# Dilated attention on one TensorE: projection steps paced by an estimate of each half slot's work, instruction pins from the first slot, and later merge pieces

## The chip, the cores and the metric

The kernel runs on 1 core of one Trainium2 chip. The metric is the time of one execution in microseconds (us). Three timed runs of the kernel before gave 2720.28, 2725.63 and 2730.9 us; the median is 2725.63.

The engines by the names of the profile: PE is TensorE (matrix products and transposes), PEld its weight loads, DVE is VectorE, ACT is ScalarE, POOL is GpSimd, and SP is the engine whose queue issues most transfers.

## The reference, cut to what matters

Two layers of a decoder trunk, on 1024 positions by 1024 features in f32. Layer 0 mixes tokens with a gated MLP, layer 1 with the attention below; each is followed by a dense MLP. The change lies in the attention: 16 heads of 64 features and three patterns (window, dilation), whose outputs are weighted by a softmax over their log sums.

```python
B_PATTERNS = ((128, 1), (512, 4), (2048, 16))
def dilated_branch(q, k, v, window, dilation, slopes):
    ...
    s = jnp.einsum('bnqrhe,bnkrhe->bnrhqk', qb, kb, preferred_element_type=jnp.float32) * (E ** -0.5)
    ...
    s = s + bias
    s = jnp.where(valid[None, :, None, None], s, NEG)
    m = jnp.max(s, axis=-1, keepdims=True)
    p = jnp.exp(s - m)
    l = jnp.sum(p, axis=-1, keepdims=True)
    o = jnp.einsum('bnrhqk,bnkrhe->bnqrhe', p / l, vb.astype(jnp.float32))
    lse = (m + jnp.log(l))[..., 0].transpose(0, 1, 4, 2, 3)
    ...
def mixer_b(h, w_qkv, w_out, slopes):
    qkv = (h @ w_qkv).reshape(B, S, N_PAT, 3, B_HEADS, B_HEAD_DIM)
    ...
    wts = jax.nn.softmax(jnp.stack(lses, axis=0), axis=0)[..., None]
    o = jnp.sum(wts * jnp.stack(outs, axis=0), axis=0)
    return o.reshape(B, S, B_HEADS * B_HEAD_DIM).astype(h.dtype) @ w_out
```

## The kernel before, in words

Every f32 operand of a product is split into a high and a low part, and a product is three matmuls (high by high, high by low, low by high). `split` casts the high part on ACT and subtracts the low part on DVE.

The stages follow one another: the gated MLP, an MLP, `values` (all value projections and those q and k that go through memory, L1338), `attention`, its output projection `go_on`, and the last MLP. `attention` works on 8 pairs of heads, and in each pair on the patterns 2, 1, 0 in this order: 24 groups, with a name such as `sc_0_1` or `pv_2_0` for pattern 0 or 2.

The order of work is written out by hand. `slots` is a table of 202 slots of two half slots each, 16 half slots a group. `at(slot, pos, rank)` and `in_half(half_slot, rank)` put closures in. The loop at the end of `attention` walks the half slots and runs what stands there. For one group these are:

- `scores` (L1553): 6 to 24 small matmuls into two `sc` banks, one for each head; two banks of each of the kinds `sc`, `pv`, `mm` and `tr` exist;
- `soften` (DVE: adds the bias and takes the row's extreme, into `p` and `stat`) and `exponentials` (ACT);
- `transposes` (L1612, L1615) into a `tr` bank; `halve` (ACT, `pThi`) and `low` (DVE, `pTlo`), its split;
- `weighted` (L1644): products with the values into a `pv` bank; `gather` (ACT) and `join` (DVE) bring it into `oT` and free the bank;
- `statistics` (L1684 to L1693): stores `stat` to memory (`st_dram`).

For each pair `merge` then reads the statistics back (`read`, L1705, into `mst`), forms the weights (`factors`, `weights`, L1732 to `w_dram`), loads them spread over the partitions (`spread`, L1739, `bc`), and scales, adds and splits the three `oT` in twelve pieces, two halves each. Pairs 0 to 5 store the result in `o_dram` (L1766). `rows_first` (L1809) and `rows_second` (L1816) load it again for the output projection, whose first steps (`out_begin`, L1829) run in the last slots, six for every eight half slots, from slot `last_group - 8` on.

Between the slots' own work the loop puts steps of `project()`: one step is three matmuls of 512 columns (L1455), 384 steps in all, that make q and k of pattern 2 and k of pattern 1 for the coming groups from the layer's input. `load` fetches a weight (L1432, `wq_raw`, `wk_raw`, two buffers), `cut` splits it (`wqk_hi` on ACT, `wqk_lo` on DVE), and a finished block is split into `qhi`, `qlo`, `khi`, `klo` one half slot later. 40 lead steps run ahead of the first slot. Then a credit gives (368 - 40)/326, about 1.006 step for each of the first 326 half slots, whatever stands in them, and 16/25 of a step for each one after.

While `in_order[0]` is true, instructions that go through `V` (DVE) and `A` (ACT) are pinned: they run in the order in which the program writes them. PE, SP and POOL are left to a scheduler that places each instruction when its inputs are ready by its own model. `in_order[0]` is set ahead of the lead steps.

## Time and profile before

| | |
|---|---|
| median of three runs | 2725.63 us (2720.28 to 2730.9) |
| the profiled execution | 2721.97 us, span 2720.3 us |
| mean granted TensorE clock | 0.993 |
| PE busy | 2653.1 us (98%), 13194 matmuls |
| DVE, ACT busy | 2016.9 us (74%), 1394.3 us (51%) |
| attention: first projection matmul to last weighted sum | about 1460 to 2022 us of the span |

A share of the whole span says little about a stage that takes a fifth of it. For this change the rows to read are those of the attention alone: the idle time of PE stretch by stretch, the waits behind it, and the clock in each stretch. A timeline row gives the start, the duration of one instruction or of a run of equal ones (x12), and in brackets the idle time just before it with the instruction that ended it. Matmuls are pipelined, so what one costs is the distance from its start to the next start, not its own duration.

### The profile page before, as it was taken

The page shows a single profiled execution, that of the slowest core. Times are in us where ns is not written, and L with a number is a line of the kernel's source. Part 1 is how long each engine was busy: PE and PEld are TensorE (multiplying, and loading weights), DVE is VectorE, ACT ScalarE, POOL GpSimd, SP SyncE. Part 2 cuts the span into 40 slices and gives each one's busy share as a digit, 9 for nine tenths or more (in the row PEclk, how much of TensorE's full clock was granted, in tenths as well). Part 3 has the DMA queues.
Part 4 walks back from the last instruction along what each step waited for, and adds up shares of the span by engine and source line. Part 5 has one row for each costly group of instructions (what it writes and reads, how often), then busy time and mean ns, then how long its engine had stood idle before and what let it go on. Part 6 is the DMA issues. An engine that isn't in the chain of part 4 may idle for free.

```text
span 2720.3 us, 37241 instructions
## 1 busy us (share of the span) xinstructions
PE 2653.1 (98%) x13194; PEld 2191.1 (81%) x13194; DVE 2016.9 (74%) x3652; ACT 1394.3 (51%) x2621; POOL 130.5 (5%) x211
## 2 busy tenths in 40 slices
PE   6999999999999999999999999999999999999998
PEld 5788888888888877888887888888787888878887
DVE  6787697877888778666663677777768966577887
ACT  3354475555444464444443677777645655544332
POOL 1000000000000001111111000000010000000000
PEclk9999999999999999999999999999999999999999
DMA  7534346677967756666646366667892654495562
GB/s 264 161 120 131 116 141 213 224 224 249 341 223 250 240 166 199 240 216 220 213 170 195 109 172 174 167 172 186 253 224 90 213 186 158 148 315 184 171 208 87
DMA packets 342223, 525.76 MB, mean 193 GB/s; under 512 B 52572, under 2 KB 169732, under 8 KB 342036
## 3 DMA queue, kind: packets, MB, share of 16 engines
q1 hardware_dynamic: 323060, 455.21, 53.2%
q0 software_dynamic: 18976, 68.17, 6.8%
q8 instruction: 104, 1.70, 0.3%
q14 instruction: 83, 0.68, 0.1%
HBM read 376.93 MB, written 146.36 MB: 192 GB/s over the span
## 4 chain that ended last, share of the span: by engine, by line
PE 66%; DVE 12%; issue 11%; DMA 6%; ACT 4%; POOL 1%; SPq 0%; DVEq 0%; POOLq 0%; ACTq 0%
PE psv L1338 15%; PE psd L972 11%; PE psua L813 8%; PE psk L1455 5%; PE psuc L813 4%; DMA adaw<-in_ada_w_dram 3%; PE psd_wout L404 3%; PE psq L1455 3%; PE psu L383 3%; PE sc L1553 3%; PE pv L1644 3%; DVE adaacc L51 2%; PE psub L813 2%; PE psv L485 1%; PE pT L1612 1%
## 5 line engine op out<-in xcount | busy, mean ns | idle before, releaser
L813 PE MATMUL psua<-right,left 128*128 128x512 f32 x1536 | 365.7, 392 | 0.1
L972 PE MATMUL psd<-rhi,lhi 128*128 128x512 f32 x896 | 350.3, 391 | 3.0 <-ACT part L51 3.0
L972 PE MATMUL psd<-rlo,lhi 128*128 128x512 f32 x896 | 350.0, 391 | 0.2
L972 PE MATMUL psd<-rhi,llo 128*128 128x512 f32 x896 | 349.6, 390 | 0.0
L813 PEld LDWEIGHTS psua<-right,left 128*128 128x128 f32 x1536 | 288.9, 189 | 61.7 <-DVE right L51 1.2
L51 ACT ACTIVATE p<-p,stat 128x128 f32<-128x128 f32 (+1 forms) x384 | 169.5, 443 | 68.1 <-DVE stat L51 67.0
L972 PEld LDWEIGHTS psd<-rhi,lhi 128*128 128x128 f32 x896 | 169.0, 189 | 39.0 <-ACT part L51 3.9
L972 PEld LDWEIGHTS psd<-rlo,lhi 128*128 128x128 f32 x896 | 168.8, 188 | 35.7 <-DVE rlo L51 1.1
L972 PEld LDWEIGHTS psd<-rhi,llo 128*128 128x128 f32 x896 | 168.9, 189 | 35.5
L813 PE MATMUL psuc<-right,left 128*128 128x512 f32 x768 | 187.1, 390 | 0.0
L51 DVE TENSOR_TENSOR pTlo<-pT,pThi 128x512 fp32r<-128x512 f32 (+1 forms) x160 | 99.5, 622 | 102.4 <-ACT pThi L51 101.0
L51 DVE SCALAR_TENSOR_TENSOR adaacc<-adaw,silu_c,adaacc 128x512 f32<-128x512 f32 x168 | 128.6, 774 | 56.1 <-DMA adaw<-in_ada_w_dram 55.0
L813 PEld LDWEIGHTS psuc<-right,left 128*128 128x128 f32 x768 | 143.6, 188 | 29.8 <-DVE right L51 0.2
L51 ACT ACTIVATE part<-part 128x512 f32<-128x512 f32 x224 | 141.4, 632 | 49.8 <-DVE part L51 44.6
L51 DVE TENSOR_TENSOR left<-ws,left 128x512 fp32r<-128x512 f32 x128 | 87.8, 687 | 73.8 <-ACT left L51 72.0
L51 DVE TENSOR_TENSOR llo<-lraw,lhi 128x1024 fp32r<-128x1024 f32 x112 | 136.3, 1217 | 2.2 <-ACT lhi L51 2.2
L1455 PE MATMUL psk<-form_L,wqk_hi 128*128 128x512 f32 x384 | 131.0, 422 | 0.0
L51 ACT CAST left<-ws 128x512 fp32r<-128x512 f32 x128 | 79.1, 620 | 96.8 <-DVE ws L51 96.6
L51 ACT CAST lhi<-lraw 128x1024 fp32r<-128x1024 f32 x112 | 117.3, 1047 | 10.5 <-PE psd L972 3.3
L51 ACT CAST pThi<-pT 128x512 fp32r<-128x512 f32 (+1 forms) x160 | 84.6, 529 | 72.8 <-PE pT L1612 57.6
L1338 PE MATMUL psv<-vrhi,form_S 128*128 128x512 f32 x384 | 120.1, 391 | 1.8 <-DVE vpart L51 0.9
L1338 PE MATMUL psv<-form_S,vrhi 128*128 128x512 f32 x384 | 118.3, 389 | 0.0
(322 smaller groups left out, 6093.4 us busy)
## 6 DMA issues: line engine op xcount, KB each, us to landing
lraw<-forms SPq DMA_DIRECT2D x112, 512.0 KB
adaw<-in_ada_w_dram SPq DMA_DIRECT2D x192, 256.0 KB
up<-in_mlp_w_up_dram SPq DMA_DIRECT2D x64, 512.0 KB
forms<-s SPq DMA_DIRECT2D x128, 256.0 KB
rraw<-in_mlp_w_down_dram SPq DMA_DIRECT2D x64, 512.0 KB
vraw<-in_b_w_qkv_dram SPq DMA_DIRECT2D x50, 512.0 KB
forms<-part SPq DMA_DIRECT2D x96, 256.0 KB
v<-vs POOLq DMA_DIRECT2D x48, 512.0 KB, 4.5
```

Of the source, the lines that this page charges most:

```text
L51: ins = call(*a, **k)
L383: T.matmul(dst, s[a], m[b], start=(n == 0), stop=(n == last))
L404: T.matmul(p[:], stat[a][:, k, o : o + P], u[b][:, w], start=n == 0, stop=n == count - 1)
L485: T.matmul(sums[u, half][:], units[u][a_][:, k * P : (k + 1) * P], hT[half][b_][:, k, :], start=k == 0 and a_ + b_ == 0, stop=k == KD - 1 ...
L813: T.matmul(acc, w[:, a, k, :], right[p][:, b, k, :], start=p in (1, 2, 5) and k + a + b == 0, stop=k == 3 and a == 1, skip_group_check=True)
L972: ins = T.matmul(sums[kind, m][:], l[a][:, k, m * P : (m + 1) * P], r[b][:, k, :], start=p in (1, 5, 2, 3) and kp + k + a + b == 0, stop=k ...
L1338: T.matmul(acc, rows[:, m * P : (m + 1) * P], cols_, start=p in (1, 2, 5) and kp + k + a + b == 0, stop=kp == 1 and k == 1 and a == 1, ski ...
L1455: T.matmul(p[:], wu[a][:, k * P : (k + 1) * P], h_op(k, half, b), start=k + c_ == 0, stop=k == KD - 1 and c_ == 2)
L1553: T.matmul(banks[e][:, sl], q_[a][rows, tq], k_[b][rows, keys], start=c_ == 0, stop=c_ == 2)
L1612: T.transpose(pst[:, o : o + P], probs[t][:, P : 2 * P] if has[t] else probs[t][:, 0:P], ident[:])
L1644: T.matmul(pvs[b][:, q0 % HALF : q0 % HALF + w_], stt, x_[:, o_ : o_ + w_], start=not begun[b], stop=left[b] == 0, skip_group_check=True)
```

## The change

Four things change, all in `attention`; no instruction is added or removed.

1. The steps' pace. `scores`, `transposes` and `weighted` add an estimate of their TensorE time to `spent[0]` as they are written. Each half slot adds 1.325 less `spent[0]` to the credit, and a step costs 0.7: heavy half slots get no step or one, light ones two.
2. `in_order[0]` is set behind the lead steps, so the lead's casts and subtracts aren't pinned.
3. In `merge`, `read` moves from slot `base + 1` to `base + 2`, `spread` from `base + 6` to `base + 8`, and each split becomes two pieces, "high" (ACT) and "low" (DVE and the store); the pieces' half slots are a new list, and for pair 6 they begin two half slots later.
4. `rows_first` and `rows_second` move three half slots earlier.

```diff
--- before.py
+++ after.py
@@ -1411,6 +1411,7 @@
             def h_op(k, half, part):
                 return form[f"L{1 if half else 2}{1 + k // 4}"][:, part, k % 4, :]
 
+            spent = [0.0]
             late = []
 
             def leave():
@@ -1540,6 +1541,7 @@
                             G.tensor_scalar(st["bias"][:], (far if g == 2 else near)[:],
                                             -8.0 * DILATION[g] * 2.0 ** (-8.0 * (h + 1) / N_HEADS), 1.0, ALU.mult, ALU.mult)
                     banks, used, spans = [bank("sc", f"sc_{2 * hp + e}_{g}_{m}") for e in range(2)], 0, []
+                    spent[0] += 0.29 + sum(0.42 if has[t] else 0.35 for t in groups[m])
                     for t in groups[m]:
                         w = 2 * P if has[t] else P
                         sl = slice(used, used + w)
@@ -1609,6 +1611,7 @@
                     def transposes(m, h=h, probs=probs, packs=packs, pT=pT):
                         pst = bank("tr", f"pT_{h}_{g}_{m}")
                         for t, nxt, o in packs[m]:
+                            spent[0] += 0.11 * (1 + nxt)
                             T.transpose(pst[:, o : o + P], probs[t][:, P : 2 * P] if has[t] else probs[t][:, 0:P], ident[:])
                             end = o + P
                             if nxt:
@@ -1630,6 +1633,7 @@
 
                     def weighted(m, e=e, h=h, rows=rows, packs=packs, pT=pT, pvs=pvs, st=st):
                         begun, left = st["begun"], st["left"]
+                        spent[0] += 0.1 + sum(0.114 * (1 + nxt) for _, nxt, _ in packs[m])
                         for t, nxt, o in packs[m]:
                             stt = my["v"][:, t, 2 * e : 2 * e + 2, :].rearrange("p a c -> p (a c)")
                             for x_ in pT[m]:
@@ -1698,7 +1702,7 @@
                 base = 8 * (3 * hp + 3)
                 box = {}
 
-                @at(*((base + 1, 1) if hp < N_PAIRS - 1 else (base - 1, 0)))
+                @at(*((base + 2, 1) if hp < N_PAIRS - 1 else (base - 1, 0)))
                 def read():
                     box["st"] = st = qp.tile([P, 3, 2, 16], F32, name=f"mst_{hp}", tag="mst", bufs=1)
                     for g in range(3):
@@ -1731,7 +1735,7 @@
                     for g in range(3):
                         nc.sync.dma_start(w_dram[hp, g].rearrange("e (q n) -> q e n", n=NT), a[:, g].rearrange("p (e n) -> p e n", n=NT))
 
-                @at(*((base + 6, 1) if hp < N_PAIRS - 1 else (base + 1, 1)))
+                @at(*((base + 8, 1) if hp < N_PAIRS - 1 else (base + 1, 1)))
                 def spread():
                     for g in (1, 2, 0):
                         bc = box[g] = row_bc(f"bc_{hp}_{g}")
@@ -1760,18 +1764,21 @@
                         hi, lo = (box[i][:, w].bitcast(F32R) for i in (2, 1))
                     else:
                         hi, lo = (t[:, hp, :] for t in ending["oT"][half])
-                    split(hi, lo, box[0][:, w])
+                    if g == "high":
+                        A.copy(hi, box[0][:, w])
+                        return
+                    V.tensor_tensor(lo, box[0][:, w], hi, op=ALU.subtract)
                     if hp < N_PAIRS - 2 and half:
                         for i in range(2):
                             nc.sync.dma_start(o_dram[hp, :, i, :], box[2 - i][:])
 
-                pieces = ((scale, 2), (scale, 1), (scale, 0), (add, 2), (add, 1), (cut, 0))
+                pieces = ((scale, 2), (scale, 1), (scale, 0), (add, 2), (add, 1), (cut, "high"), (cut, "low"))
                 if hp == N_PAIRS - 1:
                     ending["merge"] = [lambda f=f, g=g, half=half: f(g, half) for half in range(2) for f, g in pieces]
                     return
                 steps = [lambda f=f, g=g, half=half: f(g, half) for f, g in pieces for half in range(2)]
                 for n, f in enumerate(steps):
-                    in_half(2 * base + ((23, 25, 29, 31, 35, 36, 39, 40, 43, 47, 49, 53)[n] if hp < N_PAIRS - 2 else n + 22), 4)(f)
+                    in_half(2 * base + ((25, 29, 31, 35, 36, 39, 40, 43, 47, 48, 49, 50, 51, 54)[n] if hp < N_PAIRS - 2 else n + 24), 4)(f)
 
             for hp in range(N_PAIRS):
                 oTs = {}
@@ -1801,14 +1808,14 @@
             for k, half_slot in ((0, -64), (1, -56), (3, -48), (2, -38), (4, -33), (7, 11), (5, 17), (6, 18)):
                 in_half(2 * last_group + half_slot, 4)(lambda k=k: load_unit(k))
 
-            @at(last_group - 9, 0)
+            @at(last_group - 11, 1)
             def rows_first():
                 ending["oT"] = [act_pair("oTs_0")]
                 for i, t in enumerate(ending["oT"][0]):
                     for c in range(3):
                         nc.sync.dma_start(t[:, 2 * c : 2 * c + 2, :].bitcast(F32), o_dram[2 * c : 2 * c + 2, :, i, 0:HALF].rearrange("k p t -> p k t"))
 
-            @at(last_group - 8, 1)
+            @at(last_group - 9, 0)
             def rows_second():
                 ending["oT"].append(act_pair("oTs_1"))
                 for i, t in enumerate(ending["oT"][1]):
@@ -1867,19 +1874,20 @@
 
             stream = project()
             lead, credit = 5 * KD, 0
-            in_order[0] = True
             for n in range(lead):
                 leave()
                 next(stream)
+            in_order[0] = True
             due = 0
             for n, slot in enumerate(slots):
                 for half_of, pos in enumerate(slot):
                     for _, f in sorted(pos, key=lambda x_: x_[0]):
                         f()
                     leave()
-                    credit += (368 - lead) * 25 if 2 * n + half_of < 326 else 16 * 326
-                    while credit >= 326 * 25:
-                        credit -= 326 * 25
+                    credit += 1.325 - spent[0]
+                    spent[0] = 0.0
+                    while credit >= 0.35:
+                        credit -= 0.7
                         next(stream, None)
                     if n >= last_group - 8:
                         due += 6
```

What that does to the order shows at three places. The first is ACT at the start of the attention. `qs` are splits of the last blocks of `values` (from PSUM banks `psv` or sums `vpart`), `wqk_hi` the casts of the first projection weights; + marks the order after, - the order before:

```order
 L51 CAST qs_1_4_2_11876<-psv_0_1_2_11474 128x512
+L51 CAST wqk_hi<-wq_2_raw 128x1024
+L51 CAST wqk_hi<-wk_2_raw 128x1024
 L51 CAST qs_1_4_3_11892<-psv_0_1_3_11491 128x512
 L51 CAST qs_1_3_0_11909<-vpart_1_6_0_11685 128x512
 L51 CAST qs_1_3_1_11926<-vpart_1_6_1_11703 128x512
 L51 CAST qs_1_3_2_11943<-vpart_1_6_2_11724 128x512
+L51 CAST wqk_hi<-wk_1_raw 128x1024
+L51 CAST wqk_hi<-wq_2_raw 128x1024
 L51 CAST qs_1_3_3_11960<-vpart_1_6_3_11742 128x512
-L51 CAST wqk_hi<-wq_2_raw 128x1024
-L51 CAST wqk_hi<-wk_2_raw 128x1024
```

The first two weight casts no longer stand behind all `qs` casts but ahead of the last five, and two further weight casts stand ahead of the last one.

The second is TensorE in the middle of the attention, behind the score block `sc_0_1` of the third pair. Before:

```order
L1553 MATMUL sc_0_1_14489<-bk_1_14328,bq_1_14326 128x256
L1455 MATMUL psk_2_0_14433<-form_L_8626,wqk_hi 128x512 x2
L1455 MATMUL psk_2_0_14433<-form_L_8626,wqk_lo 128x512
L1644 MATMUL pv_1_0_14510<-pThi_1_0_14457,v_1_14109 128x256
L1644 MATMUL pv_1_0_14510<-pTlo_1_0_14458,v_1_14109 128x256
L1644 MATMUL pv_1_0_14510<-pThi_1_0_14457,v_1_14109 128x128
L1644 MATMUL pv_1_0_14510<-pTlo_1_0_14458,v_1_14109 128x128
```

After:

```order
L1555 MATMUL sc_0_1_14532<-bk_1_14363,bq_1_14361 128x256
L1648 MATMUL pv_1_0_14550<-pThi_1_0_14497,v_1_14130 128x256
L1648 MATMUL pv_1_0_14550<-pTlo_1_0_14498,v_1_14130 128x256
L1648 MATMUL pv_1_0_14550<-pThi_1_0_14497,v_1_14130 128x128
L1648 MATMUL pv_1_0_14550<-pTlo_1_0_14498,v_1_14130 128x128
L1456 MATMUL psk_1_1_14422<-form_L_8187,wqk_hi 128x512 x2
L1456 MATMUL psk_1_1_14422<-form_L_8187,wqk_lo 128x512
```

The half slot of a score block gets no projection step now, so the weighted sum follows the scores directly and the step comes behind it. The step itself is of another weight (`psk_1_1` against `psk_2_0`), as the paces differ.

The third is TensorE where the projection ends. Before, its last matmuls stand in the last pair, behind transposes and weighted sums of its pattern 2 and ahead of `sc_1_0` of pattern 1:

```order
L1455 MATMUL psk_1_0_18375<-form_L_8626,wqk_hi 128x512 x2
L1455 MATMUL psk_1_0_18375<-form_L_8626,wqk_lo 128x512
L1644 MATMUL pv_2_0_18541<-pThi_2_0_18494,v_2_18246 128x128
L1644 MATMUL pv_2_0_18541<-pTlo_2_0_18495,v_2_18246 128x128
```

After, they stand in pair 6, behind `sc_0_2` and ahead of the score block `sc_0_3` of its pattern 0:

```order
L1456 MATMUL psk_1_0_18081<-form_L_8626,wqk_hi 128x512 x2
L1456 MATMUL psk_1_0_18081<-form_L_8626,wqk_lo 128x512
L1648 MATMUL pv_1_1_18187<-pThi_1_3_18182,v_1_17698 128x256
L1648 MATMUL pv_1_1_18187<-pTlo_1_3_18183,v_1_17698 128x256
L1648 MATMUL pv_1_1_18187<-pThi_1_3_18182,v_1_17698 128x128
L1648 MATMUL pv_1_1_18187<-pTlo_1_3_18183,v_1_17698 128x128
L1555 MATMUL sc_0_3_18229<-bk_3_18148,bq_3_18146 128x256
```

So the stretch from there to `sc_1_0` of the last pair, about 20 half slots, has no projection step any more, and the output projection's steps begin where they did.

## The prediction

> **What bounds the kernel now.** The page's first part says it: busy time, share of the span and instructions per engine.
>
> ```profile
> PE 2653.1 (98%) x13194; PEld 2191.1 (81%) x13194; DVE 2016.9 (74%) x3652; ACT 1394.3 (51%) x2621; POOL 130.5 (5%) x211
> ```
>
> TensorE (PE) is the bound; the change leaves its 13194 matmuls as they are, so it can only take away TensorE's idle time and slow spells, or add to them. All that it moves lies in the attention, which runs from the last value projection to the last weighted sum. I cut that part into stretches with the windows view: length, busy time by engine (PE, PEld, DVE, ACT, POOL), granted clock, DMA share, GB/s.
>
> ```profile
> 1457.80:2022.00 564.20, 555.46 (x3817) 466.48 (x3818) 400.14 (x1275) 380.11 (x1134) 32.54 (x58) 0.99 0.66 182
> 1460.30:1463.80 3.50, 3.50 (x9) 2.77 (x10) 2.34 (x2) 0.81 (x1) 2.30 (x3) 0.56 0.90 269
> 1500.00:1920.00 420.00, 417.69 (x2964) 352.86 (x2963) 319.63 (x1031) 297.34 (x905) 20.07 (x40) 1.00 0.61 169
> 1927.40:1968.00 40.60, 37.53 (x270) 31.12 (x269) 27.11 (x101) 27.71 (x89) 1.40 (x4) 0.96 0.83 264
> 1951.50:1955.00 3.50, 3.50 (x13) 3.12 (x14) 3.28 (x23) 2.62 (x13) 0.11 (x1) 0.52 0.78 283
> 1962.00:2022.00 60.00, 59.05 (x377) 48.78 (x376) 36.24 (x106) 40.01 (x110) 8.24 (x10) 1.00 0.91 227
> ```
>
> In 564.20 us TensorE idles 564.20 - 555.46 = 8.74 us, and in two spells it is busy at about half its clock: 3.50 x (1 - 0.56) = 1.5 us and 3.50 x (1 - 0.52) = 1.7 us are lost there. So **11.9 us, 0.44% of the kernel, is all the idle time and lost clock that the attention has**. The waits of PE name the pieces (total, times, longest):
>
> ```profile
> PE pv L1644 <- DVE oT L51: 3.2, 7, 1.2
> PE psq L1455 <- ACT wqk_hi L51: 2.4, 1, 2.4
> PE sc L1553 <- DVE klo L51: 0.9, 1, 0.9
> PE sc L1553 <- DMA bk<-qk: 0.6, 1, 0.6
> ```
>
> 2.4 us lie at the start, 420.00 - 417.69 = 2.3 in the 420 us of the middle, 40.60 - 37.53 = 3.1 in the 40 us before the last pair's second pattern, and 60.00 - 59.05 = 0.95 behind it. I now price the change at these four places.
>
> **Start: the pins begin behind the lead steps (-3.9).** The timeline (start, duration, engine, what, idle before and its releaser):
>
> ```profile
> 1460.21 1.22 PE L1455 MATMUL psq<-form_L,wqk_hi 128*128 128x512 f32 x2 [2.42 <-ACT wqk_hi L51]
> ...
> 1447.91 0.59 ACT L51 CAST qs<-psv 128x512 fp32r<-128x512 f32 x1 [2.33 <-DMA qk<-qs]
> 1458.59 0.62 ACT L51 CAST qs<-vpart 128x512 fp32r<-128x512 f32 x1 [2.10 <-DVE vpart L51]
> 1459.12 1.04 ACT L51 CAST wqk_hi<-wq_raw 128x1024 fp32r<-128x1024 f32 x1
> 1460.19 1.23 DVE L51 TENSOR_TENSOR wqk_lo<-wq_raw,wqk_hi 128x1024 fp32r<-128x1024 f32 x1 [0.25 <-ACT wqk_hi L51]
> 1416.86 0.37 SPq L1432 DMA_DIRECT2D wq_raw<-in_b_w_qkv_dram  x1
> ```
>
> The first projection matmul waits 2.42 us for a cast of 1.04 us that is pinned behind the last `qs` cast, though its weights were asked for at 1416.86. In the changed order the first two wqk_hi casts stand on ACT directly ahead of the `qs` cast of 1447.91, where ACT idled 2.33 us; 2 x 1.04 = 2.1 fits, and DVE idles beside it. The 2.42 us go. The half clock of 1460.30 to 1463.80 begins right behind that idle, so I let its 1.5 us go too. What is late next: the two further casts now stand ahead of the last `qs` cast and can hold it by up to 2 x 1.04, less the 2.10 that ACT idled there: nothing reaches PE, since the blocks made of that `qs` are read by scores far later. Bounds: -3.9, and 0 if another cast takes the place.
>
> The Trainium skill, "TensorE: Matmul & The Clock Gate", Part 1 ("What's actually happening" and "HAM oscillation"), has the clock fall to a half after an idle window of about 3.4 us, and warns only of gaps longer than that. By that rule the 2.42 us gap would not be what halved the clock, and the sum would end 1.5 us higher. The row agrees with the half clock and its length of some 3.4 us, but shows it behind 2.42 us, and the spell of 1951.50 begins behind a gap of 1.23 (row of 1950.16 below).
>
> **Middle: steps chosen by what a half slot leaves (-0.1).** Idle time first: 2.3 us in 420 us, mostly `pv` behind the last `oT` join (the row of waits above), once on a block load, and behind it a score block once on DVE.
>
> ```profile
> 1667.69 0.98 PE L1553 MATMUL sc<-bk,bq 64*128 64x256 f32 x12 [0.63 <-DMA bk<-qk]
> 1931.53 1.32 PE L1553 MATMUL sc<-bk,bq 64*128 64x256 f32 x12 [0.22 <-DVE stat L51]
> ```
>
> Filling light half slots more and heavy ones less gives a `pv` block more matmuls between it and the join that frees its bank, but it brings score blocks closer to the softens that free theirs. I take -1.3 (half of 2.3 goes), with bounds of -2.3 and +3: one 0.22 wait as at 1931.53 in each of 8 pairs is 1.8, and a doubled block wait 0.63 more.
>
> Then the order itself has a price, inside PE's busy time: what a matmul takes depends on its neighbour.
>
> ```profile
> 1531.46 0.98 PE L1553 MATMUL sc<-bk,bq 64*128 64x256 f32 x12
> 1532.36 0.72 PE L1455 MATMUL psk<-form_L,wqk_hi 128*128 128x512 f32 x2
> 1532.93 0.39 PE L1455 MATMUL psk<-form_L,wqk_lo 128*128 128x512 f32 x1
> ...
> 1464.29 0.62 PE L1455 MATMUL psq<-form_L,wqk_hi 128*128 128x512 f32 x2
> 1464.75 0.39 PE L1455 MATMUL psq<-form_L,wqk_lo 128*128 128x512 f32 x1
> 1503.17 0.22 PE L1644 MATMUL pv<-pThi,v 128*128 128x128 f32 x1
> 1503.23 0.27 PE L1644 MATMUL pv<-pTlo,v 128*128 128x128 f32 x1
> 1503.34 0.28 PE L1644 MATMUL pv<-pThi,v 128*128 128x128 f32 x1
> 1504.02 0.68 PE L1455 MATMUL psq<-form_L,wqk_hi 128*128 128x512 f32 x2
> 1504.54 0.39 PE L1455 MATMUL psq<-form_L,wqk_lo 128*128 128x512 f32 x1
> 1927.43 0.97 PE L1553 MATMUL sc<-bk,bq 64*128 64x256 f32 x12
> 1928.34 0.39 PE L1644 MATMUL pv<-pThi,v 128*128 128x256 f32 x1
> 1928.56 0.28 PE L1644 MATMUL pv<-pTlo,v 128*128 128x256 f32 x1
> ```
>
> From start to start, a pair of projection matmuls takes 1464.75 - 1464.29 = 0.46, behind scores 0.57 (+0.11), behind `pv` 0.52 (+0.06). A `pv` takes 1503.34 - 1503.23 = 0.11, behind scores 0.22 (+0.11), and 0.06 as the first of the narrow pattern behind a projection (-0.05). In the changed order scores are followed by a projection 17 times instead of 63 and by `pv` 53 instead of 6; `pv` follows a projection 93 times instead of 143, a projection follows `pv` 116 instead of 133, and scores are entered 81 times instead of 74. So: -46 x 0.11 = -5.1; +47 x 0.11 = +5.2; -17 x 0.06 = -1.0; -50 x (0 to -0.05) = 0 to +2.5, of which I take 0.6, as only the narrow pattern's first one gains; 7 more entries into scores, which no row shows apart: 0.11 behind each and, I assume, as much ahead of it, +1.5, from 0 to double. Sum +1.2, bounds -0.9 and +4.6. Middle: -1.3 + 1.2 = -0.1.
>
> **Tail: the filler runs out earlier (+2).** Before, the last projection matmul starts at 1957.23; in the changed order it stands ahead of the last score block of pair 6, some 20 half slots earlier, while the output projection's steps still begin where they did. How much filler leaves that stretch, the same window of the projection's line (L1455) says:
>
> ```profile
> 1927.40:1968.00 40.60, 14.81 (x45) 7.95 (x45) 0.96 0.83 264
> ```
>
> 45 matmuls, at 0.46 / 2 = 0.23 each, are 10.3 us of PE. Without them PE has 37.53 - 10.3 = 27.2 us of work there, DVE 27.11 and ACT 27.71: three engines that pass each block to one another, with nothing left to hide a handover. PE's work as a whole doesn't change, so only the stretch's idle time counts: at least 27.7 - 27.2 = 0.5 us, at most all that was filled, 40.6 - 27.2 = 13.4 us. The nearest row is the same stretch with its filler, where 3.1 us still were lost and 1.7 at half clock:
>
> ```profile
> 1950.16 0.30 PE L1644 MATMUL pv<-pThi,v 128*128 128x128 f32 x1 [1.23 <-DVE oT L51]
> 1957.23 0.40 PE L1455 MATMUL psk<-form_L,wqk_lo 128*128 128x512 f32 x1
> 1960.34 0.33 PE L1553 MATMUL sc<-klo,qhi 64*128 64x128 f32 x2 [0.93 <-DVE klo L51]
> ```
>
> The 0.93 goes: the last `klo` is split long before its scores. The 1.23 waits for a join on DVE; pair 6's merge pieces, which share DVE there, start two half slots later, which I expect to move that wait rather than to remove it. I take 7 us, near the middle and above the 4.8 of before: +2, bounds -4 and +8.6. The two loads of finished rows (L1809, L1816) go out three half slots earlier each, behind pair 5's last store, which moves one half slot later; the tiles are needed only by the output projection behind 1961, so I cost them at nothing. If they do hold SP's queue, what waits behind them is the last pair's blocks, and a late block cost 0.63 us at 1667.69.
>
> **Merge's moves (0).** Its splits keep their casts (ACT) and subtracts (DVE), now in two half slots, so DVE no longer waits in order for the cast; no instruction is added. Its read stands in SP's queue behind the `st_dram` store that it waits for:
>
> ```profile
> 1655.77 0.37 SPq L1689 DMA_DIRECT2D st_dram<-stat  x1
> 1662.25 0.36 SPq L1705 DMA_DIRECT2D mst<-st_dram x1
> 1662.70 0.69 SPq L1520 DMA_DIRECT2D bq<-qk  x1
> ...
> SPq L1432 <- DVE wqk_lo L51: 69.0, 15, 13.2
> ```
>
> 6.5 us pass there and the block loads go out behind it; the 0.63 us at 1667.69 come from this. The new order keeps store, read and block loads in this sequence, so nothing goes.
>
> **The sum.** -3.9 - 0.1 + 2 = -2.0, so 2721.97 - 2.0 = 2720.0 for an execution like the profiled one. That one lies 3.7 under the median of the three runs (2725.63) and 2.7 under the mean of all four (2724.6); runs of one program differ by 10.6 us, so I add 2.7: **2723**.
>
> **The rivals.**
>
> *Every stall goes.* If DVE and ACT, relieved by merge's later pieces, keep pace without filler, the tail keeps 0.5 to 2 us and the start and middle give all: -3.9 - 2.3 + 1.2 - 4 = -9.0, so 2724.6 - 9.0 = 2716; with the switches at their lower bound, 2714. For it: no engine has more than 27.71 us there. Against it: the joins were late even with filler.
>
> *Nothing changes.* TensorE's work is conserved, and waits only change places: 2724.6. For it: 0.55% idle in the middle leaves pacing nothing to earn.
>
> *The block loads come late in every pair (slower).* In the changed SP order a `wk_raw` load stands between merge's read and the `bq`/`bk` loads. It must wait for the subtract that frees its buffer; such waits took 69.0 / 15 = 4.6 us each, and a block load had no slack at 1667.69. If that subtract comes after the read, 8 pairs lose up to 4.6 us each; with half of it covered, 8 x 2.3 = 18, or 8 x (2.3 + 1.5) = 30 if each gap also halves the clock: 2723 + 18 = 2741 to 2753. Against it: ACT's and DVE's new order has that cut earlier, so the buffer should be free. It decides once the subtract ends after the read's issue.
>
> *The tail's upper bound.* All 13.4 us idle, some with half clock behind: +8.6 to +12, 2730 to 2735.
>
> *The half clock stays.* If the spell at 1460 is not the child of the 2.42 us gap ahead of it, only the gap goes: -2.42 - 0.1 + 2 = -0.5, 2724. Against it: the spell begins within 0.1 us of the gap's end. This is what the Trainium skill's rule, named above, would give.
>
> **How the numbers follow.** Forecast 0.58, nothing changes 0.12, the half clock stays 0.05, every stall goes 0.12, tail at its bound 0.07, late blocks 0.06. Faster by over 0.5% (about what a measurement of this kernel can tell from no change) is below 2712: only all stalls gone and a low median, 0.05. Slower by over 0.5% is above 2739: late blocks and a rest, 0.06. The range runs from the first rival's lower figure, less 2 for the scatter of a median, to the tail's upper bound: 2712 to 2735.
>
> **What would show it.** Right: no idle ahead of the first psq matmul and full clock behind it; idle in 1500 to 1920 still near 1 to 3 us; 5 to 9 us of PE waits on DVE or ACT between pair 6's third score block and pair 7's second pattern. Wrong: that stretch at under 2 or over 12 us idle; a wait of scores on bk in most pairs; psq still behind wqk_hi.

## The result and the profile after

Seven runs of each kernel: **2735.54 us after (2731.51 to 2741.49), 2725.69 us before (2716.19 to 2730.9)**. The ratio is 1.004, 95% interval [1.002, 1.0059]: slower by 0.4%, some 10 us. The prediction said 2723, a few us faster, with a range up to 2735.

The profiled execution took 2731.51 us, 9.5 more than the one of before. TensorE's six largest waits in the changed kernel's attention (total, times, longest):

```profile
PE pv L1648 <- DVE oT L51: 4.3, 5, 1.7
PE sc L1555 <- DMA bk<-qk: 3.9, 2, 3.0
PE pT L1615 <- DVE pTlo L51: 2.7, 3, 1.0
PE pT L1615 <- ACT p L51: 1.7, 1, 1.7
PE pv L1648 <- ACT pThi L51: 1.2, 2, 1.0
PE sc L1555 <- DVE stat L51: 1.1, 1, 1.1
```

The wait of psq for wqk_hi (2.4 us) is gone. Three kinds are new, the two of pT and that of pv for pThi; three have grown: bk was 0.6 us, the join `oT` 3.2, `stat` 0.2. The windows say where: the middle of the attention, all of it (1451.40 is the last value projection, 2033.10 the last weighted sum), and two half-clock spells, stretches in which the granted clock is 0.50; the columns are those of the windows in the prediction.

```profile
1500.00:1920.00 420.00, 409.38 (x2883) 346.27 (x2881) 308.85 (x989) 288.96 (x869) 17.53 (x36) 0.99 0.57 159
1451.40:2033.10 581.70, 563.68 (x3818) 473.65 (x3816) 399.81 (x1275) 379.06 (x1133) 32.33 (x59) 0.98 0.63 175
1815.70:1819.10 3.40, 3.40 (x16) 3.05 (x14) 2.56 (x12) 2.51 (x9) 0.00 (x0) 0.50 0.19 56
1969.30:1979.50 10.20, 10.20 (x51) 8.71 (x52) 5.41 (x23) 6.10 (x18) 0.00 (x0) 0.50 0.87 283
```

In the same 420 us of the middle TensorE idles 420.00 - 409.38 = **10.6 us, against 2.3 before**. The attention takes 581.7 us against 564.3 (from 1457.4, the last value projection of before, to 2021.7). Of the 17.4 us that it is longer, idle time is 18.0 - 8.7 = 9.3. The clock record has four half-clock spells in the attention, 20.4 us in all, against 6.8; half of the difference, 6.8, is lost. Some 1.3 remain for the order of matmuls. The rest of the execution was 8.0 us shorter than in the profile of before, 6.05 of it ahead of the attention, where both programs are the same; the profile of before has half-clock spells of 6.8 and 3.4 us there (at 422.3 and 975.3) that this one lacks, and near the start one of 3.4 where this one has 6.8, so that 3.4 us of the 6.05 are clock. So the 17.4 us of this one execution are more than the 10 of the medians.

Three waits, each in its place. First the pv block at 1813.99 on TensorE, and what ACT and DVE did ahead of it:

```profile
1813.99 0.33 PE L1648 MATMUL pv<-pThi,v 128*128 128x128 f32 x1 [1.71 <-DVE oT L51]
...
1810.45 0.56 ACT L51 CAST khi<-psk 128x512 fp32r<-128x512 f32 x1
1810.91 1.04 ACT L51 CAST wqk_hi<-wk_raw 128x1024 fp32r<-128x1024 f32 x1
...
1811.04 0.69 DVE L51 TENSOR_TENSOR klo<-psk,khi 128x512 fp32r<-128x512 f32 x1 [1.79 <-ACT khi L51]
1811.99 1.23 DVE L51 TENSOR_TENSOR wqk_lo<-wk_raw,wqk_hi 128x1024 fp32r<-128x1024 f32 x1 [0.26 <-ACT wqk_hi L51]
1813.25 0.69 DVE L51 TENSOR_TENSOR oT<-oT,pv 64x512 f32<-64x512 f32 x1
```

The join `oT` (1813.25) would free the pv bank. DVE stood idle for 1.79 us ahead of it, but it is pinned behind `klo` and `wqk_lo`, and these wait for ACT's casts. In the kernel before, this join (the 56th of 96 in both) ran at 1807.21, and the same `klo` and `wqk_lo` (the 24th and the 20th of their kind in both) stand behind the join two further on, with no wait:

```profile
1807.21 0.69 DVE L51 TENSOR_TENSOR oT<-oT,pv 64x512 f32<-64x512 f32 x1 [0.21 <-ACT oT L51]
...
1819.68 0.67 DVE L51 TENSOR_TENSOR oT<-oT,pv 64x512 f32<-64x512 f32 x1
1820.28 0.68 DVE L51 TENSOR_TENSOR pTlo<-pT,pThi 128x512 fp32r<-128x512 f32 x1
1820.88 0.67 DVE L51 TENSOR_TENSOR klo<-psk,khi 128x512 fp32r<-128x512 f32 x1
1821.48 1.21 DVE L51 TENSOR_TENSOR wqk_lo<-wk_raw,wqk_hi 128x1024 fp32r<-128x1024 f32 x1
```

Nothing of this is in the slots' table. The splits of a finished block and of a weight ride on the projection's stream, and the new pace moved the stream against the pairs. The other two waits lie in the tail. One is for a late block load. The other is for an exponential of ACT (`p`), and what held that shows two engines further back:

```profile
1941.09 0.98 PE L1555 MATMUL sc<-bk,bq 64*128 64x256 f32 x12 [3.01 <-DMA bk<-qk]
...
1967.66 0.33 PE L1615 MATMUL pT<-ident,p 128*128 128x128 f32 x1 [1.70 <-ACT p L51]
...
1966.78 0.24 ACT L51 ACTIVATE ma<-ma 128x48 f32<-128x48 f32 x1 [1.99 <-DVE ma L51]
...
1965.98 0.18 DVE L51 TENSOR_TENSOR mm<-mst 128x16 f32<-128x16 f32 x1 [1.52 <-DMA mst<-st_dram]
...
1957.44 0.33 SPq L1691 DMA_DIRECT2D st_dram<-statT  x1
1964.04 0.36 SPq L1709 DMA_DIRECT2D mst<-st_dram  x1
```

`mm` and `ma` are merge's `factors`. They are pinned too, and they wait for merge's read of pair 6, which SP issued 6.6 us after the store; before it was 4.6 us (1944.18 to 1948.74), and DVE didn't wait for it.

### The profile page after: what moved, and what is told of

The parts are those of the page before. It is cut to its first block, busy times and chain, and to the rows that moved or that the text cites. A ratio compares the mean times of both kernels' runs of the same rounds, so it can differ in the third digit from the quotient of the medians.

```text
span 2729.7 us, 37238 instructions
## 1 busy us (share of the span) xinstructions
PE 2654.0 (97%) x13194; PEld 2194.7 (80%) x13194; DVE 2017.2 (74%) x3652; ACT 1394.2 (51%) x2621; POOL 129.6 (5%) x211
## 5 line engine op out<-in xcount | busy, mean ns | idle before, releaser
L51 DVE CUSTOM_DVE_ANT_0 p<-sc,bias 128x128 f32<-128x128 f32 (+1 forms) x384 | 113.1, 345 | 10.2 <-PE sc L1555 9.8
```

The costliest lines, as they stand in the source:

```text
L51: ins = call(*a, **k)
```

## The experiments

Every kernel here computes all that the reference asks. Ratios are to the kernel before, run on the same chip beside them, with 95% intervals; "idle" is 420.00 less PE's busy time in the window 1500 to 1920 of the one profiled execution. "In phase" means that the stream's step count stays within 2 steps of the old pace's at every half slot; the counts are worked out from the code's numbers. Three further runs ("cut later" and the two at the end) stand in the text alone.

| run | pace of the steps | phase against the old pace | last step, half slot | idle | ratio |
|---|---|---|---|---|---|
| before | even, 1.006 | - | 350 | 2.3 | 1 |
| after | by estimate | up to 13 ahead | 330 | 10.6 | 1.004 [1.002, 1.0059] |
| pins alone | even | in phase | 350 | 1.8 | 0.9985 [0.9975, 0.9996] |
| after, old pace | even | in phase | 350 | 0.8 | 0.9981 [0.9972, 0.999] |
| pins and new pace | by estimate | up to 13 ahead | 330 | 8.8 | 1.005 [1.0037, 1.0064] |
| rows back | by estimate | up to 13 ahead | 330 | 9.7 | 1.005 [1.0036, 1.0064] |
| merge back | by estimate | up to 13 ahead | 330 | 9.7 | 1.0056 [1.004, 1.0071] |
| late end | by estimate | 8 ahead to 9 behind | 350 | 10.4 | 1.0017 [1.0007, 1.0028] |
| even, early end | even, 1.04 | from 0 to 13 ahead | 330 | 6.1 | 1.0007 [0.9997, 1.0016] |
| scores only | by scores | 3 ahead to 5 behind | 347 | 10.7 | 1.0042 [1.0022, 1.0061] |
| others only | by the rest | 8 ahead to 7 behind | 350 | 9.2 | 1.0036 [1.0022, 1.0051] |
| two or none | 2, 0, 2, 0 | in phase | 350 | 1.7 | 0.9968 [0.9958, 0.9978] |
| six ahead | even, 1.006 | 6 ahead | 350 | 12.8 | 1.0067 [1.0055, 1.0079] |
| estimate in phase | by estimate | in phase | 349 | 1.5 | 0.998 [0.9969, 0.9992] |

**Which part does it?** One part undone in the changed kernel, three times; then one part alone, and two.

`rows_first` and `rows_second` at their old slots:

```diff
-            @at(last_group - 11, 1)
+            @at(last_group - 9, 0)
             def rows_first():
...
-            @at(last_group - 9, 0)
+            @at(last_group - 8, 1)
```

> The changed kernel with one part undone: rows_first and rows_second stand where they stood before. Theory: the loss has three sources at different places (finished rows loaded ahead of a block load in the last pairs; merge's casts ahead of a pattern's first pThi; the weight cut ahead of a join). In the changed kernel's profile a score block waits 3.01 us for bk at 1941.09, and the clock halves at 1942.0 for 3.4 us; this run takes away that one, 3.0 + 1.7 = 4.7 us: about 2731 beside the changed kernel's 2735.5 and 0.2% over the kernel before, no wait of scores on bk over 1 us in pair 6, and the waits at the pair boundaries still there. Rival (the pace alone does it, by leaving DVE and ACT too little time between a pair's stages): the wait moves to another instruction in the same stretch, and the time stays at 2735.

1.005: nothing is won. The wait for bk stands at 5.07 us, so the rows' place in the table doesn't cause it.

The old pace, all else as changed:

```diff
-                    credit += 1.325 - spent[0]
-                    spent[0] = 0.0
-                    while credit >= 0.35:
-                        credit -= 0.7
+                    credit += (368 - lead) * 25 if 2 * n + half_of < 326 else 16 * 326
+                    while credit >= 326 * 25:
+                        credit -= 326 * 25
```

> The changed kernel with the old pace of the projection steps; pins, merge and rows as changed. Theory: the waits on a join behind a weight cut go (1.71 at 1813.99 and 1.34 at 1881.96, each with 1.7 at half clock behind it, 6.4 in all), and most of the single ones (1.11, 0.92, 0.44); the waits of pT behind merge's casts at pair boundaries (0.96, 1.02, 0.75) and the late bk stay in some form: 2735.5 - 9 = 2726, about the kernel before. Rival (the pace alone does it): also the tail's 6 us idle and 6.8 us at half clock go and the start's gain stays: 2735.5 - 17 = 2719, below the kernel before by 0.2 to 0.3%.

0.9981, a gain over the kernel before. The first theory, three sources, falls; the pace is the whole loss. PE in the middle:

```profile
1500.00:1920.00 420.00, 419.17 (x2987) 355.83 (x2987) 321.91 (x1032) 298.05 (x902) 19.29 (x38) 1.00 0.61 170
```

Merge as before (`base + 1`, `base + 6`, the undivided `split`, the old twelve half slots):

> The changed kernel with merge as before (read, spread, pieces and the undivided cut); pins, pace and rows as changed. Theory: the waits of pT on pTlo at the start of a pair's pattern 2 (0.96 at 1617.59, 1.02 at 1684.29, 0.75 + 0.31 at 1751.51) go, and the rest stays: 3 us, about 2732. Rival (the pace alone does it): 2735 or more, since merge's pieces at their old places now meet another pace.

1.0056. At two of the three places where pT waited behind merge's casts only 0.2 us are left, at the third 0.68. The tail's wait behind merge's read is gone too, but others came (1.33 us for bk at 1600.14, and 1.04 at 1961.90 with 6.8 us of half clock), and the time didn't follow.

The kernel before with only the pins moved:

```diff
-            in_order[0] = True
             for n in range(lead):
                 leave()
                 next(stream)
+            in_order[0] = True
```

> The kernel before with one part of the change: the pins begin behind the lead steps. Both theories: no wait of the first psq matmul and full clock behind it, 2.4 + 1.5 = 3.9 us: 2722 beside 2725.7 and a ratio of 0.9986; all else as before. If the half clock comes anyway, 2.4.

0.9985, 4 us, and no wait of psq. And the pace without the other two parts, by undoing both edits above:

> The kernel before with the pins behind the lead and the new pace alone; merge and rows as before. The first four runs said that the pace alone makes the kernel slower. Then this one is as slow as the whole change: a ratio of 1.004 to 1.006, attention some 580 to 586 us long (564.3 before, 581.7 in the changed kernel), with a wait for bk of 2.5 to 5 us in pair 6 and 1.7 and 1.3 us behind weight cuts. If the pace needs the other parts to do harm, the ratio is under 1.002.

1.005: the pace needs no help to do harm.

**What in the pace?** It ends the projection early, it spreads steps unevenly, and it shifts where the splits fall.

```diff
-                    credit += 1.325 - spent[0]
+                    credit += 1.285 - spent[0]
```

> The changed kernel with 1.285 in place of 1.325 in the pace's budget, so that the projection ends at half slot 350 as before, and not at 330; the spread over heavy and light half slots stays. Theory E (the early end does it: the finished rows' tiles come free sooner, their loads go out ahead of the block loads, and the tail lacks filler): the 3.0 us wait for bk in pair 6 and the half clock in the tail go, 5 to 9 us, ratio about 1.001. Theory S (the spread does it: half slots of scores without a step bring banks round sooner than DVE and ACT free them): the waits in the middle, 11 us of idle ahead of pair 6's last block less those 3.0 and some 3.4 at half clock, stay: ratio 1.003 or more.

1.0017, in the middle still 10.4 us idle: each theory has half. The bk wait of pair 6 is gone, and so is the one behind merge's read. The gain on the changed kernel isn't clear of noise, as the intervals overlap ([1.0007, 1.0028] and [1.002, 1.0059]). The counterpart, an even pace that ends early, `credit += 339 * 25` in each half slot:

> The changed kernel with an even pace of 1.04 step in each half slot, so that the projection ends at half slot 330 as in the changed kernel, without the spread by estimate. Theory E: a wait for bk of 2.5 to 5 us in pair 6 and half clock in the tail as in the changed kernel: 6 to 9 us above the run with the old pace (0.9981), ratio 1.001. Theory S: as good as the run with the old pace, 0.998, idle in the middle at about 2 us.

1.0007 is the figure of theory E, but not by its path: there is no wait for bk in pair 6, and 6.1 us are idle in the middle. An even pace of 1.04 also runs ahead, by 13 steps at its end. The tail has the wait behind merge's read, 1.82 us with 10.2 us of half clock behind it. Next, `cut(i + 1)` and `load(i + 3)` at `k == 2` instead of ahead of the matmuls:

> The changed kernel with each weight's cut (and the load behind it) two steps later in the stream. If the weight cut, pinned ahead of a join on DVE, is what holds the pv bank at 1813.99 and 1881.96 (1.71 and 1.34 us, with 1.7 at half clock behind each), both go: 6.4 us, ratio 1.0016, unless another pair's cut then meets a join. If they stay, DVE is late there for another reason.

The 1.71 and 1.34 us waits and their half-clock spells did go, but others of 0.5 to 0.7 us came in other pairs, idle in the middle was 7.1 us, and the ratio stayed at 1.004 [1.0027, 1.0053]. The cut was the cause of those two waits, not of the time as a whole.

Then the estimate was halved. Without the lines of `transposes` and `weighted`, with 0.94 in place of 1.325:

> The changed kernel, with only the scores counted in the estimate (budget 0.94 for each half slot): half slots of scores get no step, all others an even share; the stream stays within 5 steps of the old pace through all pairs and ends at half slot 347. Runs so far: even pace and late end 0.9981, even and early end 1.0007, spread and late end 1.0017, spread and early end 1.004. Theory S (a score half slot without a step brings the next bank round before DVE and ACT freed it): 1.001 to 1.002, with 8 to 10 us of idle in the middle. Theory P (what costs is the phase: the spread makes the stream run 5 to 8 steps ahead of the old pace in the first pair and drift from there, so that weight cuts and splits, pinned on ACT and DVE, fall ahead of joins and pTlo): 0.998, with 2 to 4 us idle.

And without the line of `scores`, with 1.04:

> The counterpart: only transposes and weighted sums counted (budget 1.04), scores not; nearly every half slot gets a step, but the stream is 5 to 8 steps ahead of the old pace in the first pair and 5 behind it by the seventh, and ends at half slot 350. Theory S: 0.998 to 0.999. Theory P: 1.001 to 1.002, with waits of pv and pT of 0.5 to 1.7 us behind a weight cut in several pairs.

1.0042 and 1.0036: both cost as much as the whole, and neither theory foretold both. If the phase is the cause, five steps off the old place are enough. The first run has one wait of 13.39 us in the last pair besides. So the spread and the phase were changed one at a time. Two steps or none, in phase, on the kernel with the pins alone:

```diff
-                    credit += (368 - lead) * 25 if 2 * n + half_of < 326 else 16 * 326
+                    credit += 2 * (1 - half_of) * ((368 - lead) * 25 if 2 * n + half_of < 326 else 16 * 326)
```

> The kernel with the pins alone (ratio 0.9985, 3.9 us idle before the last projection matmul), with the same number of steps in two half slots as before, but both in the first and none in the second; the stream is never more than one step off its old place, and ends where it did. Theory S, widened by the last two runs (a half slot without a step lacks the cover between what ACT and DVE make in one half slot and TensorE uses in the next, whichever half slot it is): 8 to 11 us idle before the last projection matmul, ratio 1.001 to 1.003. Theory P (only the phase of weight cuts and splits costs): 0.9985 and 4 us idle.

And an even pace, six steps ahead:

```diff
-            for n in range(lead):
+            for n in range(lead + 6):
...
-                    credit += (368 - lead) * 25 if 2 * n + half_of < 326 else 16 * 326
+                    credit += (368 - lead) * 25 if 2 * n + half_of < 326 else 10 * 326
```

> The kernel with the pins alone, with 46 lead steps instead of 40 and the same even pace behind them; the last ten steps are spread so that the stream ends as before. Every half slot has its step, only the phase of cuts and splits against the pairs is six steps ahead. Theory S: 0.9985, 4 us idle before the last projection matmul. Theory P: 1.001 to 1.003, 8 to 11 us idle, with waits of pv on a join or of pT on pTlo at the same place in each pair.

0.9968 and 1.0067. Half slots without a step cost nothing, even half of all; six steps of phase cost 0.8% over the pins alone, more than twice what theory P had put. The windows, two or none first, then six ahead:

```profile
1500.00:1920.00 420.00, 418.35 (x2998) 360.38 (x2995) 327.38 (x1044) 302.00 (x912) 19.88 (x40) 1.00 0.62 176
```

```profile
1500.00:1920.00 420.00, 407.24 (x2817) 339.87 (x2816) 308.36 (x982) 285.83 (x861) 17.58 (x36) 1.00 0.57 161
```

Idle time is not all of it. The attention as a whole, six ahead first, then the pins alone:

```profile
1449.50:2036.80 587.30, 566.30 (x3819) 471.80 (x3818) 402.68 (x1278) 380.21 (x1133) 32.37 (x59) 0.99 0.62 174
1452.00:2020.20 568.20, 556.53 (x3819) 467.22 (x3818) 399.47 (x1276) 379.16 (x1134) 32.47 (x59) 0.99 0.65 180
```

Of the 19.1 us between them 9.3 are idle time. PE's busy time grew by 9.8, of which 1.7 are half clock. The other 8.1 have no cause shown: the order on TensorE changed too (733 changes of kind, that is of the sort of matmul from one to the next, against 706), and no run parts that from the waits.

With six ahead the waits come back once in each pair, 68 to 70 us apart, here on scores, and DVE shows the cause ahead of the first of these three: a weight's cut in front of the soften that frees the score bank.

```profile
1638.89 0.59 PE L1553 MATMUL sc<-khi,qhi 64*128 64x256 f32 x2 [0.87 <-DVE stat L51]
1706.86 0.59 PE L1553 MATMUL sc<-khi,qhi 64*128 64x256 f32 x2 [0.42 <-DVE stat L51]
1776.26 0.59 PE L1553 MATMUL sc<-khi,qhi 64*128 64x256 f32 x2 [0.70 <-DVE stat L51]
...
1636.46 0.69 DVE L51 TENSOR_TENSOR qlo<-psq,qhi 128x512 fp32r<-128x512 f32 x1 [1.06 <-ACT qhi L51]
1637.40 1.23 DVE L51 TENSOR_TENSOR wqk_lo<-wk_raw,wqk_hi 128x1024 fp32r<-128x1024 f32 x1 [0.26 <-ACT wqk_hi L51]
1638.55 0.28 DVE L51 CUSTOM_DVE_ANT_0 p<-sc,bias 128x128 f32<-128x128 f32 x1
```

Last, the whole change with its estimate tied to the old phase:

```diff
-                    credit += 1.325 - spent[0]
+                    even += (368 - lead) / 326 if 2 * n + half_of < 326 else 0.64
+                    credit += 1.05 - spent[0] - 0.2 * (made - even)
```

> The changed kernel with its estimate, but tied to the even pace: what the stream is ahead of the even count is taken from the credit (a fifth of a step's lead in each half slot), so that it never leaves the old place by more than 2 steps and ends at half slot 349; 90 half slots still get no step and 89 two (76 and 89 in the changed kernel). Theory P (the phase of cuts and splits is what costs): idle before the last projection matmul falls from 13.6 to about 4 us and the ratio from 1.004 to 0.996 to 0.9985. Theory S (half slots without a step): 1.0017 as with the late end alone.

0.998, with 90 of the first 326 half slots without a step:

```profile
1500.00:1920.00 420.00, 418.51 (x2985) 356.46 (x2984) 324.05 (x1038) 300.28 (x909) 19.17 (x38) 1.00 0.61 172
```

**A faster version.** With the pins alone the last pair waited for a block load behind a read that waits for its store:

```profile
1996.29 1.65 PE L1553 MATMUL sc<-bk,bq 64*128 64x256 f32 x12 [5.49 <-DMA bk<-qk]
...
1979.79 1.25 SPq L1689 DMA_DIRECT2D st_dram<-stat  x1
1988.21 0.36 SPq L1705 DMA_DIRECT2D mst<-st_dram  x1
1988.67 0.57 SPq L1520 DMA_DIRECT2D bq<-qk  x1
```

SP's block loads and merge's reads were pinned in program order (`tc.keep_in_program_order` around the two `dma_start`):

> The kernel before with the pins behind the lead, and on SP the block loads and merge's reads pinned in program order, so that no read that waits for a store stands ahead of a bq or bk load. In the run with the pins alone (ratio 0.9985) the last pair waited 5.49 us for bk, whose load stood behind such a read, with 6.8 us of half clock behind it. If that wait comes in most executions, it goes: 5.5 + 3.4 = 9 us, ratio 0.9955 to 0.9975. If it was one execution's, or the next late transfer takes its place (the v loads, 6.33 us in the run with the old pace), 0.998 to 0.9985.

0.9981 [0.9969, 0.9992], no gain over the pins alone (0.9985) that the intervals show: a wait of 3.16 us for a block load stayed, at another block. Two steps or none and this order of SP, together:

> The two fastest edits so far together, on the kernel before with the pins behind the lead: two steps in one half slot and none in the next (0.9968; 574 changes of kind on TensorE instead of 706, its start-to-start sum 551.5 us instead of 556.0), and SP's block loads and merge's reads in program order (0.9981). If the late bk load in the last pair (5.17 us in the run with two or none) is cut as before, to about 3 us and less half clock: 0.995 to 0.9965. If late transfers merely change places there: 0.9968.

**0.9961 [0.9947, 0.9975]**, 2708.98 us beside 2718.0: the lowest ratio of all. Its interval overlaps that of two or none alone ([0.9958, 0.9978]), so what SP's order adds isn't shown.

## Why the prediction was wrong, point by point

By the two profiled executions the terms came out as -4.1 at the start, +1.3 for the order, +11.7 in the middle and +8.4 in the tail, in place of -3.9, +1.2, -1.3 and +2.

- **Start (-3.9).** Right, in both halves: the pins alone gave a ratio of 0.9985 [0.9975, 0.9996], 4 us, and the half clock went with the gap. It lasted from 1459.9 to 1463.3 (window 1459.90:1463.30, clock 0.51), so it began in the last 0.3 us of the gap and not just behind it.
- **Price of the order (+1.2).** Right in size, as far as a remainder tells: 1.3 us are what idle time and half clock leave in the changed kernel. Its single terms weren't measured. The number of changes of kind alone doesn't give it: the changed kernel has 655 against 706 and lost, two or none has 574, and its matmuls' start-to-start sum without the idle time fell from 556.0 (pins alone) to 551.5 us.
- **Middle, idle time (-1.3).** This step failed. "Filling light half slots more and heavy ones less gives a `pv` block more matmuls between it and the join that frees its bank" counted TensorE's side of the half slot only. The step's other work, a cast of 1.04 and a subtract of 1.23 us for each weight and 0.6 and 0.7 for each finished block, sits in ACT's and DVE's pinned order at the half slot where the stream happens to be. The upper bound of +3 repeated a wait of 0.22 (its terms make 2.4); measured were +8.3 us idle, and two half-clock spells behind 1.71 and 1.34 us waits, 3.4 more. The prediction did see that the cut comes earlier in ACT's and DVE's order, but only in the rival of late blocks, as a buffer freed in time; what then stands behind the cut on DVE it put at nothing.
- **Tail (+2, bounds -4 and +8.6).** Mis-sized: from 1938 to 1969 TensorE idled 6.4 us, and spells of 3.4 and 10.2 us at half clock cost 6.8: 13.2 against 4.8 before, +8.4. That this lies within the bounds is luck: they were made of handovers between three engines without filler, but the two largest waits were for a late block load (3.01) and, through ACT and DVE, for merge's read (1.70).
  - The block load: the loads of finished rows were costed at nothing; in the changed kernel SP issues one of them for 4.12 us ahead of pair 6's block loads. But with their place put back the bk wait stayed. In pair 6, one of 2.4 us or more came in every run of the estimate that ended early, and in none that ended late or had an even pace. Which of the two, the estimate or the early end, makes SP put them first is open.
  - Late transfers aren't the new pace's alone. Every experiment whose projection ends at half slot 347 or later has one wait of 1.84 to 13.39 us in the last pair (5.49 with the pins alone, 6.33 with the old pace), which the profile of before lacks. So +8.4, from one execution of each kernel, is no firm price.
- **Merge's moves (0).** Right in the time, within the measurement: undone, 1.0056 [1.004, 1.0071] beside 1.004 [1.002, 1.0059]. Not right in the path: the prediction kept the sequence of store, read and block loads and so put the later read at nothing, but the pinned `factors` waited for it. That wait came in the runs that had both the moved read and an early end (after, rows back, even early end, cut later: 0.55 to 1.82 us) and in none that lacked one of the two.
- The rival of late blocks foresaw a wait in every pair, at 18 to 30 us in all, but named a load on SP. In the middle the waits were mostly for DVE, and the loss was 10 us by the medians.
- The mean of the four executions is 2724.7, not 2724.6; nothing hangs on it.

That phase, and not half slots without a step, makes the loss in the middle is shown (six ahead, two or none, estimate in phase). How the loss follows from the number of steps isn't: an even pace that drifts from 0 to 13 ahead idled 6.1 us in the middle, a steady six ahead 12.8. An early end was not tried apart from the phase, as a stream that ends early is ahead of its old place.

## What to carry to other kernels

When filler work is paced by what one engine has free, list what else each filler step issues on the other engines; if those run in a fixed order, the place of the filler is part of that order, and a pace that drifts moves it. Change the spread of such work and its phase one at a time: here the phase alone lost 0.8%, and the spread alone lost nothing (two or none 0.9968, the estimate in phase 0.998, the even pace 0.998 to 0.9985). Grouping filler steps by two, each group where the old steps were, saves changes of kind on TensorE; 0.9968 beside 0.9985 is a gain at the edge of the noise.

## What the runs showed of the hardware

- In the changed kernel's attention, gaps of 1.71, 1.34, 3.01 and 1.70 us were each followed within 2 us by a half clock of 3.4 us or more (10.2 behind the last), while gaps of 1.11 and 1.02 us were not. By the rule of the Trainium skill weighed in the prediction ("TensorE: Matmul & The Clock Gate", Part 1, "HAM oscillation") none of the four would; the runs speak against it.
- But no length of gap divides the two cases. With merge back a gap of 1.72 us (at 1812.74) was followed by full clock, and with six ahead one of 0.69 (at 1827.57) by 3.4 us of half clock. One and the same gap, in a stretch that both programs share, went both ways, the kernel before first:

```profile
975.58 1.11 PE L236 MATMUL pst<-ident,acc 128*128 128x128 f32 x4 [1.48 <-ACT h L51]
975.30:978.70 3.40, 3.12 (x10) 2.64 (x11) 2.88 (x6) 2.31 (x4) 0.00 (x0) 0.51 0.53 143
...
971.54 0.66 PE L236 MATMUL pst<-ident,acc 128*128 128x128 f32 x4 [1.47 <-ACT h L51]
971.50:974.90 3.40, 3.36 (x17) 2.84 (x18) 2.84 (x7) 2.08 (x3) 0.00 (x0) 1.00 0.58 153
```

- So half-clock spells in stretches that all programs share come in one execution and not in the next (422.3 and 975.3 us in the profile of before, neither in that of after). These two, 6.8 and 3.4 us long, cost some 5 us: one profile can differ from another by that alone.
